# A hybrid attention encoder: tensor work of its projections moved from GpSimd to VectorE, buffers and one product order changed

## The chip, the cores and the metric

The kernel runs on one core of a Trainium2 chip. The metric is device time of one execution, in microseconds (us); the runs shown are whole executions, and one further execution was profiled. Engines are called PE (TensorE), DVE (VectorE), ACT (ScalarE), POOL (GpSimd) and SP (SyncE, which issues nearly all DMAs).

## The reference

One pre-norm layer with two parallel mixers, all in fp32. What the kernel's first stage has to produce is the projection of 2048 prompt rows and 128 sample rows (8 streams of 16):

```python
h = rms_norm(x, g_in)
proj = jnp.einsum('btd,de->bte', h, w_in)
qa, ka, va, z_a, qd, ckv_in, kpe_in, z_b, m_a, m_b = jnp.split(proj, SPLIT_POINTS, axis=-1)
qa = rope(qa.reshape(b, t, H_A, 2, DK_A), pos)
k_rows = rope(ka.reshape(b, t, H_A, 2, DK_A), pos).reshape(b, t, H_A, 2 * DK_A)
# y_a = W_oa(DiffAttn * silu(z_a)), y_b = W_ob(MLA * silu(z_b))
# x   = x + W_out(sigmoid(m_a) * y_a + sigmoid(m_b) * y_b)
```

Differential attention has 4 heads, latent attention (MLA) 4 heads; the sample streams attend to 2048 cached rows each.

## The kernel before, in words

Every fp32 operand of a matmul is split in two numbers of TensorE's faster fp32 format (`hi`, by an ACT cast, and `lo = x - hi`, by a subtraction, L113 to L115), and each product is three matmuls, hi by hi, hi by lo and lo by hi.

Five stages follow one another on PE: `_phase_a` (projections, 0 to 662 us), `_phase_a2` (latent and rope work with the gate products z, to about 950), `_phase_b` (prompt attention, to about 1850), `_sample` (the 8 sample streams, to about 2260) and `_phase_c` (output projections y and out, to the end).

Phase A treats the 2176 rows as three parts of 768, 768 and 640 columns of h transposed. For each part:
- `squares` and `factors`: six (five) loads of x rows (`xn`), ACT squares with sums, POOL turns the sums into `rs`, DVE makes diagonals `dg` (L187), and PE spreads them with a matrix of ones into bank `psr` (L188). ACT copies that to R. For parts 1 and 2 the squares are issued inside the first pairs of the part before, the factors after its pair number 7 (counted from 0).
- `load_part`: 16 tiles of xT are scaled by R (L202, DVE), cast (`xhi`, L204, ACT) and split (`xlo`, L205, POOL).
- `sums`: four differences of x blocks for the seven-product scheme (L215, DVE), each split into `S[0..3]` (L217 ACT, L218 DVE, for one of the four POOL).
- `v_block` (psv, 144 matmuls for 6 row tiles) and `kpe_block`.
- eleven pairs, in the order latent, then rope and gate four times, then two latents. A pair multiplies a 2 by 2 block of weights with a 2 by 2 block of h by seven products p1 to p7 of 12 matmuls each. `pair_weights` loads weights, makes four sums (L294, POOL, in part 0 only; they are stored to `wsum` in DRAM and loaded from there in parts 1 and 2) and splits the seven operands. `pair_products` adds the banks up on DVE (L325): v from p6, m1 from p2, u3 from p7, v and w from p5, v from p3, u3 from p4, in this order. A rope pair ends with four products by cosine and sine per half, two on POOL (L355, L357) and two on DVE (L356, L358).

Seven banks of PSUM rotate through these products, so a product may start when the adds on the bank seven allocations earlier are done. Temporaries come from one rotating pool `tmp` (12 buffers and some lent by another pool); the `dg` tiles are among them. The weight sums have one buffer (pool `a_q`). All engines run their instructions in the order in which a scheduler put them, from a cost model and priorities given by the order of the code; on each engine that order is fixed when the kernel is built.

In `_sample`, `diff_stream(b)` handles differential attention of stream b, `mla_streams(b)` latent attention of streams b and b+1; the last gate products z_13 to z_15 are placed between their matmuls. Names there: `ssd`, `atsd`, `posd`, `otsd` belong to a diff stream, `ktsm`, `ssm`, `posm`, `otsm` to MLA streams. Phase C starts with `y`, from `o` tiles that are loaded to `ox` and split.

Of the kernel before, what the change touches and what calls it, by code (L numbers as in the profile page):

```python
# [11 lines left out]
F32 = mybir.dt.float32  # L12
F32R = mybir.dt.float32r
BF16 = mybir.dt.bfloat16
AF = mybir.ActivationFunctionType
ALU = mybir.AluOpType
# [4 lines left out]
P = 128  # L21
D = 1024
SEQ = 2048
NB = 8
# [5 lines left out]
H = 4  # L30
# [6 lines left out]
NG = 384  # L37
GROUPS = [(t, min(NG, T - t)) for t in range(0, T, NG)]

PARTS = [(0, 384), (768, 384), (1536, 320)]  # L40
# [88 lines left out]
def _phase_a(c):  # L129

    nc, tc = c.nc, c.tc
    with (
        tc.tile_pool(name="a_h", bufs=1) as ph,
        tc.tile_pool(name="a_w", bufs=7) as pw,
        tc.tile_pool(name="a_s", bufs=2) as pst,
        tc.tile_pool(name="a_q", bufs=1) as pq,
        tc.tile_pool(name="a_t", bufs=12) as pt,
        tc.tile_pool(name="a_c", bufs=1) as pc,
        tc.tile_pool(name="a_p", bufs=7, space=PSUM) as pp,
# [13 lines left out]
        def tmp(n, name, m=P):  # L153
            return turn("t", 4, pt, c.zt).tile([P, NG], F32, tag="t", name=name)[:m, :n]
# [6 lines left out]
            [(c.zh if i == 0 else ph).tile([P, 4, 2 * NG], F32R, tag=f"{l}{i}", name=f"x{l}{i}") for l in ("hi", "lo")]  # L161
            for i in range(2)
        ]
        S = [[ph.tile([P, 4, NG], F32R, name=f"t{l}{i}") for l in ("h", "l")] for i in range(4)]

        R, ss = {}, {}

# [8 lines left out]
        def factors(p):  # L176
            t0, n = PARTS[p]
            nt = 2 * n // P
            R[p] = pc.tile([P, 2 * NG], F32, tag="R", name=f"R{p}", bufs=2)
            r = pc.tile([P, 8], F32, tag="rs", name=f"rs{p}", bufs=2)[:, :nt]  # L180
            _rsqrt(c, r, ss[p][:, :nt], 1.0 / D)
            for a in range(0, nt, 3):
                w = min(3, nt - a) * P
                ps = bank(f"psr{p}_{a}")
                for t in range(a, min(a + 3, nt)):
                    dg = tmp(P, f"dg{p}_{t}")
                    nc.vector.tensor_scalar(dg, c.ident, r[:, t : t + 1], None, op0=ALU.mult)  # L187
                    nc.tensor.matmul(ps[:, (t - a) * P : (t - a + 1) * P], c.ones, dg, start=True, stop=True)  # L188
                nc.scalar.copy(R[p][:, a * P : a * P + w], ps[:, :w])
            nc.sync.dma_start(c.Rh[:, t0 : t0 + 2 * n], R[p][:, : 2 * n])  # L190

        def load_part(p):
            t0, n = PARTS[p]
            raw = {}
            for j in range(4):
                for i in range(2):
                    kt = j + 4 * i
                    for half in range(2):
                        cut = slice(half * n, half * n + n)
                        x = tmp(n, f"x{p}_{kt}_{half}")  # L200
                        nc.sync.dma_start(x, c.i["xT"][:, kt, t0 + half * n : t0 + half * n + n])
                        nc.vector.scalar_tensor_tensor(x, x, c.g_in[:, kt : kt + 1], R[p][:, cut], op0=ALU.mult, op1=ALU.mult)  # L202
                        hi, lo = (z[:, j, cut] for z in X[i])
                        nc.scalar.copy(hi, x)  # L204
                        nc.gpsimd.tensor_tensor(lo, x, hi.bitcast(F32), op=ALU.subtract)  # L205
                        raw[j, i, half] = x
            return raw

        def sums(p, raw):
            n = PARTS[p][1]  # L210
            for j in range(4):
                b11, b12, b21, b22 = (raw[j, i, half] for i in range(2) for half in range(2))

                for i, out, x, y in ((0, b11, b12, b11), (2, b12, b22, b12), (1, b22, b22, b11), (3, b21, b21, b22)):
                    nc.vector.tensor_tensor(out, x, y, op=ALU.subtract)  # L215
                    hi, lo = (z[:, j, :n] for z in S[i])
                    nc.scalar.copy(hi, out)  # L217
                    (nc.gpsimd if i == 2 else nc.vector).tensor_tensor(lo, out, hi.bitcast(F32), op=ALU.subtract)  # L218

        def v_block(p):  # L220
            t0, n = PARTS[p]
# [43 lines left out]
        def kpe_block(p):  # L265

            t0, n = PARTS[p]
            st = stage([P, KT, 64], f"ws_kpe{p}")
            nc.sync.dma_start(st, c.i["wkpe"])
            w = operand([P, KT, P], f"w_kpe{p}")  # L270
            _split(nc, w[:, :, 0:64], w[:, :, 64:128], st)
            for half in range(2):
                ps = bank(f"ps_kpe_{p}_{half}")[:, :n]
                for kt in range(KT):
                    xh, xl = (z[:, kt % 4, half * n : half * n + n] for z in X[kt // 4])
                    nc.tensor.matmul(ps, w[:, kt, :], xh, start=(kt == 0), stop=False)
                    nc.tensor.matmul(ps, w[:, kt, :], xl, start=False, stop=(kt == KT - 1))
                t = tmp(n, f"kpe{p}_{half}")
                nc.scalar.copy(t, ps)
                nc.sync.dma_start(c.kpT[:, t0 + half * n : t0 + half * n + n], t)  # L280

        def pair_weights(p, u, nm):
            st = [stage([P, KT, P], f"ws_{nm}_{i}") for i in range(2)]
            nc.sync.dma_start(st[0], c.i["wu"][u])
            sums = pq.tile([P, 4, 4, P], F32, tag="s", name=f"s_{nm}")
            a11, a12 = (st[0][:, k : k + 4] for k in (0, 4))
            s1, s2, s3, s4 = (sums[:, i] for i in range(4))
            if p == 0:
                nc.sync.dma_start(st[1], c.i["wu"][u + 1])
                a21, a22 = (st[1][:, k : k + 4] for k in (0, 4))  # L290
                for out, x, y, op in (
                    (s1, a21, a22, ALU.add), (s2, s1, a11, ALU.subtract), (s4, a12, s2, ALU.subtract), (s3, a11, a21, ALU.subtract)
                ):
                    nc.gpsimd.tensor_tensor(out, x, y, op=op)  # L294
                nc.sync.dma_start(c.wsum[u // 2], sums)
            else:

                a22 = st[1][:, 4:8]
                nc.sync.dma_start(sums, c.wsum[u // 2])
                nc.sync.dma_start(a22, c.i["wu"][u + 1][:, 4:8])  # L300
            ops = []
            for i, x in enumerate((a11, a12, s4, s2, s3, s1, a22)):
                w = operand([P, KT, P], f"w{i}_{nm}")
                _split(nc, w[:, 0:4], w[:, 4:8], x)
                ops.append(w)
            return ops
# [10 lines left out]
        def pair_products(p, u, nm):  # L317

            n = PARTS[p][1]
            a11, a12, s4, s2, s3, s1, a22 = pair_weights(p, u, nm)  # L320
            one, two = slice(0, n), slice(n, 2 * n)
            m1, v, u3, w = (tmp(n, f"{x}{nm}") for x in ("m1", "v", "u3", "w"))

            def add(out, x, y):
                nc.vector.tensor_tensor(out, x, y, op=ALU.add)  # L325

            p1 = product(f"p1{nm}", a11, X[0], one)
            nc.scalar.copy(m1, p1)
            p2 = product(f"p2{nm}", a12, X[1], one)
            p3 = product(f"p3{nm}", s4, X[1], two)  # L330
            p6 = product(f"p6{nm}", s2, S[1], one)
            add(v, p6, m1)
            add(m1, p2, m1)
            p7 = product(f"p7{nm}", s3, S[2], one)
            add(u3, p7, v)
            p5 = product(f"p5{nm}", s1, S[0], one)
            add(v, p5, v)
            add(w, p5, u3)
            add(v, p3, v)
            p4 = product(f"p4{nm}", a22, S[3], one)  # L340
            add(u3, p4, u3)
            return (m1, v), (u3, w)

        def rope_pair(p, u, dst, pair, out, scale):
            t0, n = PARTS[p]
            res = pair_products(p, u, f"r{u}_{p}")
            for half in range(2):
# [4 lines left out]
                co, si = cs[:, 0], cs[:, 1]  # L352
                ta, tb = res[0][half], res[1][half]
                m1, m2, m3, m4 = (tmp(n, f"m{i}{nm}") for i in range(4))
                nc.gpsimd.tensor_tensor(m1, ta, co, op=ALU.mult)  # L355
                nc.vector.tensor_tensor(m2, tb, si, op=ALU.mult)  # L356
                nc.gpsimd.tensor_tensor(m3, tb, co, op=ALU.mult)  # L357
                nc.vector.tensor_tensor(m4, ta, si, op=ALU.mult)  # L358
                nc.vector.tensor_tensor(m1, m1, m2, op=ALU.subtract)
                nc.vector.tensor_tensor(m3, m3, m4, op=ALU.add)  # L360
# [37 lines left out]
        for p in range(len(PARTS)):  # L398
            raw = load_part(p)
            sums(p, raw)  # L400
            v_block(p)
            kpe_block(p)
            for i, f in enumerate(pairs(p)):
                f()
                if p + 1 < len(PARTS):
                    if i < 2 * PARTS[p + 1][1] // P:
                        squares(p + 1, i)
                    elif i == 7:
                        factors(p + 1)


# [329 lines left out]
def _sample(c, stack):  # L741
# [215 lines left out]

    for b in range(0, NB, 2):
        diff_stream(b)
        mla_streams(b)  # L960
        diff_stream(b + 1)


    ss, r = (p1.tile([P, H * SEQ // P], F32, name=f"rsub{i}") for i in range(2))
    flat = c.rsub.rearrange("h t -> (h t)").rearrange("(p r) -> p r", p=P)
    nc.sync.dma_start(ss, flat)
    for i in range(0, H * SEQ // P, 8):
        _rsqrt(c, r[:, i : i + 8], ss[:, i : i + 8], 1.0 / P)
    nc.sync.dma_start(flat, r)

    gz = big([P, 8, TS], "s_gz")
    nc.sync.dma_start(gz, c.gzT[:, :, new].rearrange("k p n -> p k n"))
# [478 lines left out]
```

## Time and profile before

| | us |
|---|---|
| three runs, lowest, median, highest | 2659.81, 2671.47, 2674.51 |
| profiled execution | 2666.7 |
| its span in the profile | 2664.9 |

| engine | PE | DVE | ACT | POOL |
|---|---|---|---|---|
| busy us | 2453.1 | 1629.3 | 1207.0 | 813.4 |
| share of the span | 92% | 61% | 45% | 31% |

The mean granted clock of PE is 0.968 of full speed (2.4 GHz); where the profile says 0.50, it is the lower level, 1.2 GHz. Shares are means over stages with different limits: DVE is busy for 80% of the first part of phase A. The idle time of PE is read stage by stage: what PE waited for, how often and how long.

### The profile page before, as it was taken

The page shows a single profiled execution, that of the slowest core. Times are in us where ns is not written, and L with a number is a line of the kernel's source. Part 1 is how long each engine was busy: PE and PEld are TensorE (multiplying, and loading weights), DVE is VectorE, ACT ScalarE, POOL GpSimd, SP SyncE. Part 2 cuts the span into 40 slices and gives each one's busy share as a digit, 9 for nine tenths or more (in the row PEclk, how much of TensorE's full clock was granted, in tenths as well). Part 3 has the DMA queues.
Part 4 walks back from the last instruction along what each step waited for, and adds up shares of the span by engine and source line. Part 5 has one row for each costly group of instructions (what it writes and reads, how often), then busy time and mean ns, then how long its engine had stood idle before and what let it go on. Part 6 is the DMA issues. An engine that isn't in the chain of part 4 may idle for free. (4 is left out here: it accounts for less than half of the span.)

```text
span 2664.9 us, 44262 instructions
## 1 busy us (share of the span) xinstructions
PE 2453.1 (92%) x15470; PEld 2166.9 (81%) x15470; DVE 1629.3 (61%) x3358; ACT 1207.0 (45%) x2996; POOL 813.4 (31%) x996
## 2 busy tenths in 40 slices
PE   6898898999788889999999999998999997999998
PEld 5798798898787879888998998786675774888887
DVE  7686777867665557887686677896333323433333
ACT  5443543444433356666575566775334333311111
POOL 6362411311533333344343334444101001122221
PEclk9999999999899899999999999999999998999999
DMA  5777577477767796576467657423887676534432
GB/s 196 238 271 242 182 245 243 155 233 240 233 204 254 241 285 213 186 238 198 145 186 219 215 176 226 141 76 122 344 329 294 256 303 212 173 130 130 127 112 93
DMA packets 303998, 553.29 MB, mean 208 GB/s; under 512 B 29184, under 2 KB 230176, under 8 KB 288544
## 3 DMA queue, kind: packets, MB, share of 16 engines
q1 hardware_dynamic: 303776, 550.46, 62.6%
q8 instruction: 123, 2.02, 0.3%
q14 instruction: 99, 0.81, 0.1%
HBM read 397.16 MB, written 153.19 MB: 207 GB/s over the span
## 5 line engine op out<-in xcount | busy, mean ns | idle before, releaser
L100 PE MATMUL z<-z_hi,zw 128*128 128x384 f32 (+1 forms) x768 | 264.9, 345 | 35.2 <-ACT zt L453 26.4
L102 PE MATMUL z<-z_hi,zw 128*128 128x384 f32 (+1 forms) x768 | 258.4, 336 | 3.1 <-DMA zw<-wz 2.9
L101 PE MATMUL z<-z_lo,zw 128*128 128x384 f32 (+1 forms) x768 | 258.9, 337 | 0.0
L1055 DVE TENSOR_REDUCE pmd<-sd 128x1 f32<-128x512 f32 (+3 forms) x320 | 189.7, 603 | 52.5 <-PE sd L1156 31.6
L1057 ACT ACTIVATE ed<-sd,pmd 128x512 f32<-128x512 f32 (+3 forms) x320 | 200.8, 631 | 43.7 <-DVE pmd L1055 29.4
L1096 POOL TENSOR_SCALAR ed<-ed,ad 128x512 f32<-128x512 f32 (+3 forms) x160 | 114.9, 733 | 293.8 <-DVE ad L1072 134.1
L1156 PE MATMUL sd<-k,q 128*128 128x512 f32 (+2 forms) x640 | 191.6, 386 | 3.2 <-ACT ed L1057 1.5
L100 PEld LDWEIGHTS z<-z_hi,zw 128*128 128x128 f32 x768 | 148.9, 194 | 54.4 <-ACT zt L453 32.8
L102 PEld LDWEIGHTS z<-z_hi,zw 128*128 128x128 f32 x768 | 148.5, 193 | 10.1 <-issue 4.6
L101 PEld LDWEIGHTS z<-z_lo,zw 128*128 128x128 f32 x768 | 148.9, 194 | 8.1 <-issue 6.3
L115 DVE TENSOR_TENSOR zw<-zs,zw 128x512 fp32r<-128x512 f32 x128 | 91.8, 746 | 95.2 <-ACT zw L114 91.3
L1096 POOL TENSOR_SCALAR em<-em,am 128x512 f32<-128x512 f32 (+3 forms) x160 | 104.4, 667 | 141.8 <-DVE am L1072 107.3
L100 PE MATMUL y<-o,wh_ab 128*128 128x384 f32 (+1 forms) x384 | 127.8, 333 | 9.1 <-DVE sm L1277 9.1
L1280 POOL TENSOR_TENSOR sm<-sm,sm 128x384 f32<-128x384 f32 (+1 forms) x48 | 48.1, 1003 | 267.4 <-DVE sm L1277 267.4
L102 PE MATMUL y<-o,wl_ab 128*128 128x384 f32 (+1 forms) x384 | 126.8, 331 | 0.3 <-DVE wl_ab L115 0.3
L101 PE MATMUL y<-o,wh_ab 128*128 128x384 f32 (+1 forms) x384 | 127.0, 331 | 0.0
L1057 ACT ACTIVATE em<-sm,pmm 128x512 f32<-128x512 f32 (+3 forms) x160 | 100.1, 628 | 58.7 <-DVE pmm L1055 46.3
L1114 DVE TENSOR_TENSOR ptld<-ptd,pthd 128x512 fp32r<-128x512 f32 (+3 forms) x160 | 96.2, 605 | 49.5 <-ACT pthd L1113 48.8
L1277 DVE SCALAR_TENSOR_TENSOR sm<-sm,y 128x384 f32<-128x384 f32 (+1 forms) x96 | 50.4, 530 | 117.1 <-PE y L102 117.0
L1055 DVE TENSOR_REDUCE pmm<-sm 128x1 f32<-128x512 f32 (+3 forms) x160 | 95.8, 604 | 34.3 <-PE sm L1199 21.0
L1282 ACT ACTIVATE m<-sm 128x384 fp32r<-128x384 f32 (+1 forms) x48 | 24.3, 506 | 202.6 <-POOL sm L1280 202.6
L1156 PEld LDWEIGHTS sd<-k,q 128*128 128x128 f32 x640 | 104.1, 191 | 13.2 <-ACT ed L1057 4.1
(510 smaller groups left out, 7845.9 us busy)
## 6 DMA issues: line engine op xcount, KB each, us to landing
zs<-in_wu_dram SPq DMA_DIRECT2D x64, 512.0 KB
zw<-wz SPq DMA_DIRECT2D x64, 512.0 KB
ksd<-in_ckT_dram SPq DMA_DIRECT2D x32, 1024.0 KB
vsd<-in_cv_dram SPq DMA_DIRECT2D x32, 1024.0 KB
q<-Qs SPq DMA_DIRECT2D x128, 128.0 KB
wz<-zw SPq DMA_DIRECT2D x32, 512.0 KB
ksm<-in_cc_dram SPq DMA_DIRECT2D x16, 1024.0 KB
smT<-zt SPq DMA_DIRECT2D x80, 192.0 KB
```

Source lines behind the costliest of these rows:

```text
L100: nc.tensor.matmul(out, ah, bh, start=(j == 0), stop=False)
L101: nc.tensor.matmul(out, ah, bl, start=False, stop=False)
L102: last = nc.tensor.matmul(out, al, bh, start=False, stop=(j == n - 1))
L115: nc.vector.tensor_tensor(lo, src, hi.bitcast(F32), op=ALU.subtract)
L1055: nc.vector.tensor_reduce(nm_, ps[:, :w], axis=AX.X, op=ALU.max, negate=True)
L1057: nc.scalar.activation(e[:, :w], ps[:, :w], AF.Exp, bias=nm_, accum_out=l[:, s, i : i + 1])
L1096: nc.gpsimd.tensor_scalar(p, p, a[:, 0, j : j + 1], 1.0, op0=ALU.mult, op1=ALU.mult)
L1114: nc.vector.tensor_tensor(ptl[ch][:, :n, i * P : (i + 1) * P], v, hi.bitcast(F32), op=ALU.subtract)
L1156: nc.tensor.matmul(ps[:, :n], qs[s][:, j, qc], ks[s].tiles[i][:, :n], start=(j == 0), stop=(j == 1 and not last))
L1277: nc.vector.scalar_tensor_tensor(s, s, 1.0, ps, op0=ALU.add, op1=ALU.mult)
L1280: nc.gpsimd.tensor_tensor(sm[0], sm[0], sm[1], op=ALU.add)
L1282: nc.scalar.mul(z[0], sm[0], 0.5)
```

## The change

- The POOL operations of phase A (`xlo` of L205, the one `tl` of L218, the weight sums of L294, two rope products of L355 and L357) are issued on DVE: 152 instructions.
- The pool of weight sums has two buffers.
- `dg` has three tiles of its own, and factors are issued after pair 6.
- The fourth sum of x blocks has no tiles of its own: after `kpe_block`, `last_sum` writes its split over the second half of X[0]; p4 reads it there. p4 stands behind p3, ahead of p6, p7 and p5; the halves of `kpe_block` are swapped.
- At the end of `_sample` the last `mla_streams` comes after the last `diff_stream`, and the block `rsub` after the first round of streams.

```diff
-        tc.tile_pool(name="a_q", bufs=1) as pq,
+        tc.tile_pool(name="a_q", bufs=2) as pq,
...
-        S = [[ph.tile([P, 4, NG], F32R, name=f"t{l}{i}") for l in ("h", "l")] for i in range(4)]
+        S = [[ph.tile([P, 4, NG], F32R, name=f"t{l}{i}") for l in ("h", "l")] for i in range(3)]
...
-                    dg = tmp(P, f"dg{p}_{t}")
+                    dg = pc.tile([P, P], F32, tag="dg", name=f"dg{p}_{t}", bufs=3)
...
-                        nc.gpsimd.tensor_tensor(lo, x, hi.bitcast(F32), op=ALU.subtract)
+                        nc.vector.tensor_tensor(lo, x, hi.bitcast(F32), op=ALU.subtract)
...
                     nc.vector.tensor_tensor(out, x, y, op=ALU.subtract)
-                    hi, lo = (z[:, j, :n] for z in S[i])
-                    nc.scalar.copy(hi, out)
-                    (nc.gpsimd if i == 2 else nc.vector).tensor_tensor(lo, out, hi.bitcast(F32), op=ALU.subtract)
+                    if i < 3:
+                        split(out, (z[:, j, :n] for z in S[i]))
+
+        def split(src, parts):
+            hi, lo = parts
+            nc.scalar.copy(hi, src)
+            nc.vector.tensor_tensor(lo, src, hi.bitcast(F32), op=ALU.subtract)
+
+        def last_sum(p, raw):
+            n = PARTS[p][1]
+            for j in range(4):
+                split(raw[j, 1, 0], (z[:, j, n : 2 * n] for z in X[0]))
...
-            for half in range(2):
+            for half in (1, 0):
...
-                    nc.gpsimd.tensor_tensor(out, x, y, op=op)
+                    nc.vector.tensor_tensor(out, x, y, op=op)
...
-            for i, x in enumerate((a11, a12, s4, s2, s3, s1, a22)):
+            for i, x in enumerate((a11, a12, s4, a22, s2, s3, s1)):
...
             p3 = product(f"p3{nm}", s4, X[1], two)
+            p4 = product(f"p4{nm}", a22, X[0], two)
...
-            p4 = product(f"p4{nm}", a22, S[3], one)
             add(u3, p4, u3)
...
-                nc.gpsimd.tensor_tensor(m1, ta, co, op=ALU.mult)
+                nc.vector.tensor_tensor(m1, ta, co, op=ALU.mult)
                 nc.vector.tensor_tensor(m2, tb, si, op=ALU.mult)
-                nc.gpsimd.tensor_tensor(m3, tb, co, op=ALU.mult)
+                nc.vector.tensor_tensor(m3, tb, co, op=ALU.mult)
...
             kpe_block(p)
+            last_sum(p, raw)
...
-                    elif i == 7:
+                    elif i == 6:
                         factors(p + 1)
...
         diff_stream(b)
-        mla_streams(b)
+        if b < NB - 2:
+            mla_streams(b)
         diff_stream(b + 1)
-
-
-    ss, r = (p1.tile([P, H * SEQ // P], F32, name=f"rsub{i}") for i in range(2))
...
+        if b == NB - 2:
+
+            mla_streams(b)
+        if b == 0:
+
+            ss, r = (p1.tile([P, H * SEQ // P], F32, name=f"rsub{i}") for i in range(2))
```

Three places in the order of instructions (the changed file's lines of phase A behind `sums` stand ten lower: L325 has become L335). The first is PE in part 0, around the fourth rope pair, where the factors of part 1 (`psr`, from `dg`) are spread. Before:

```order
L312 MATMUL p4r_0_1886<-th_146,w_r_0_1794 128x384
L313 MATMUL p4r_0_1886<-tl_147,w_r_0_1794 128x384
L314 MATMUL p4r_0_1886<-th_146,w_r_0_1794 128x384
L188 MATMUL psr_0_1948<-dg_0_1949,ones 128x128
L188 MATMUL psr_3_1959<-dg_3_1960,ones 128x128
L312 MATMUL p1g_0_2006<-xhi_136,w_g_0_1981 128x384
L313 MATMUL p1g_0_2006<-xlo_137,w_g_0_1981 128x384
```

Changed:

```order
L322 MATMUL p5g_0_1739<-th_140,w_g_0_1650 128x384
L323 MATMUL p5g_0_1739<-tl_141,w_g_0_1650 128x384
L324 MATMUL p5g_0_1739<-th_140,w_g_0_1650 128x384
L188 MATMUL psr_0_1768<-dg_0_1769,ones 128x128
L188 MATMUL psr_0_1768<-dg_1_1772,ones 128x128
L188 MATMUL psr_0_1768<-dg_2_1775,ones 128x128
L188 MATMUL psr_3_1779<-dg_3_1780,ones 128x128
L322 MATMUL p1r_0_1826<-xhi_136,w_r_0_1801 128x384
L323 MATMUL p1r_0_1826<-xlo_137,w_r_0_1801 128x384
```

The products of `psr` stood behind the fourth rope pair and now stand ahead of it; a pair ended with p4 and now ends with p5.

The second place is DVE in part 0, where the diagonals `dg` for part 1 stand (`m0r` to `m3r` are rope products, `w_l`, `w_r` weight splits, `csr` cosine and sine). Before, at the end of the fourth rope pair:

```order
L358 TENSOR_TENSOR m3r_0_1_1927<-vr_0_1798,csr_0_1_1922 128x384
L187 TENSOR_SCALAR dg_3_1960<-ident,rs_1945 128x128
L115 TENSOR_TENSOR w_l_0_2129<-s_l_0_2116,w_l_0_2129 128x512
L115 TENSOR_TENSOR w_l_0_2132<-s_l_0_2116,w_l_0_2132 128x512
L356 TENSOR_TENSOR m1r_0_0_1903<-u3r_0_1799,csr_0_0_1900 128x384
L356 TENSOR_TENSOR m1r_0_1_1925<-wr_0_1800,csr_0_1_1922 128x384
L187 TENSOR_SCALAR dg_0_1949<-ident,rs_1945 128x128
```

Changed, in the adds of the second rope pair (`s_g` is a weight sum):

```order
L335 TENSOR_TENSOR m1r_0_1150<-p2r_0_1168,m1r_0_1150 128x384
L115 TENSOR_TENSOR w_r_0_1454<-ws_r_0_0_1441,w_r_0_1454 128x512
L187 TENSOR_SCALAR dg_0_1769<-ident,rs_1765 128x128
L187 TENSOR_SCALAR dg_1_1772<-ident,rs_1765 128x128
L187 TENSOR_SCALAR dg_2_1775<-ident,rs_1765 128x128
L335 TENSOR_TENSOR u3r_0_1152<-p7r_0_1222,vr_0_1151 128x384
L115 TENSOR_TENSOR w_r_0_1460<-ws_r_0_1_1442,w_r_0_1460 128x512
L304 TENSOR_TENSOR s_g_0_1625<-ws_g_0_1_1623 128x512
L304 TENSOR_TENSOR s_g_0_1625<-ws_g_0_0_1622,ws_g_0_1_1623 128x512
```

The first three diagonals moved forward by two rope pairs, and weight sums stand among the adds.

The third place is PE at the end of the sample streams. Before, the gate product z_15 stands among MLA matmuls:

```order
L892 MATMUL ssm_1_24020<-kTsm_1_0_24021,sp 64x512
L100 MATMUL z_15_25658<-z_hi_25076,zw_4_15_25650 128x384
L101 MATMUL z_15_25658<-z_lo_25077,zw_4_15_25650 128x384
L102 MATMUL z_15_25658<-z_hi_25076,zw_4_15_25651 128x384
L100 MATMUL z_15_25658<-z_hi_25076,zw_4_15_25650 128x384
```

Changed, it ends ahead of them:

```order
L102 MATMUL z_15_25656<-z_hi_25074,zw_4_15_25649 128x384
L870 MATMUL otsd_24177<-ident,osd_24170 128x128
L891 MATMUL ktsm_0_0_0_24193<-ident,ksm_0_0_24190 128x128 x4
L891 MATMUL ktsm_0_0_1_24199<-ident,ksm_0_0_24190 128x128 x4
L891 MATMUL ktsm_0_1_0_24208<-ident,ksm_0_1_24205 128x128 x4
L891 MATMUL ktsm_0_1_1_24214<-ident,ksm_0_1_24205 128x128 x4
```

The last z went from the MLA streams to the last diff stream, and nothing of z is left beside the MLA matmuls.

## Rows read from the trace of the kernel before

**Rows 1.** Busy time by stretch: PE, PEld, DVE, ACT, POOL; then granted clock, DMA share, GB/s.

```profile
17.00:235.00 218.00, 184.96 (x945) 174.80 (x946) 174.01 (x255) 94.97 (x192) 121.73 (x83) 0.92 0.70 233
235.00:450.00 215.00, 192.38 (x1038) 185.33 (x1037) 157.08 (x262) 93.34 (x190) 55.65 (x38) 0.96 0.66 217
450.00:662.00 212.00, 196.66 (x1181) 189.32 (x1180) 157.19 (x275) 90.46 (x191) 40.02 (x36) 0.97 0.65 214
```

**Rows 2.** Waits of PE, 0 to 662 us: total us, times, longest.

```profile
PE psr L188 <- DVE dg L187: 39.0, 3, 17.7
PE psv L236 <- ACT xhi L204: 14.3, 4, 5.9
PE p2r L312 <- DVE vg L325: 11.2, 6, 3.3
PE p3r L312 <- ACT w_r L114: 9.1, 1, 9.1
PE p2r L312 <- DVE vl L325: 6.9, 1, 6.9
PE psv L238 <- POOL xlo L205: 3.1, 1, 3.1
```

**Rows 3.** Timeline of POOL: start, duration, [idle before, releaser].

```profile
93.08 1.26 POOL L294 TENSOR_TENSOR s_r<-ws_r 128x512 f32<-128x512 f32 x1 [24.43 <-DMA wsum<-s_l]
```

**Rows 4.** Timeline of DVE in the fourth rope pair.

```profile
224.99 0.29 DVE L187 TENSOR_SCALAR dg<-ident,rs 128x128 f32<-128x128 f32 x1 [1.44 <-DMA out_kT_dram<-m2r]
```

**Rows 5.** Stretches right behind PE's gaps, PE alone: busy, count, clock.

```profile
99.10:103.10 4.00, 3.95 (x11) 0.50 0.98 317
103.10:107.10 4.00, 4.00 (x24) 0.97 0.96 358
219.30:222.30 3.00, 2.95 (x11) 0.50 0.88 260
447.50:451.50 4.00, 3.94 (x14) 0.50 0.80 252
```

**Rows 6.** Groups of POOL's instructions, 0 to 662: busy, mean ns, idle before.

```profile
L205 POOL TENSOR_TENSOR xlo<-x,xhi 128x384 fp32r<-128x384 f32 (+1 forms) x48 | 59.1, 1255 | 96.9 <-ACT xhi L204 96.9
L355 POOL TENSOR_TENSOR m0r<-m1r,csr 128x384 f32<-128x384 f32 (+1 forms) x12 | 15.4, 1280 | 180.0 <-DVE m1r L325 180.0
L294 POOL TENSOR_TENSOR s_r<-ws_r,ws_r 128x512 f32<-128x512 f32 x4 | 6.2, 1557 | 0.0
```

**Rows 7.** Groups of DVE's instructions, 0 to 662 us.

```profile
L202 DVE SCALAR_TENSOR_TENSOR x<-x,vec,R 128x384 f32<-128x384 f32 (+1 forms) x48 | 47.0, 1013 | 3.8 <-DMA x<-in_xT_dram 3.8
L215 DVE TENSOR_TENSOR x<-x,x 128x384 f32<-128x384 f32 (+1 forms) x48 | 36.3, 770 | 0.0
L115 DVE TENSOR_TENSOR w_r<-s_r,w_r 128x512 fp32r<-128x512 f32 x48 | 36.0, 761 | 42.8 <-ACT w_r L114 42.8
L356 DVE TENSOR_TENSOR m1r<-u3r,csr 128x384 f32<-128x384 f32 (+1 forms) x12 | 15.9, 1321 | 0.0
```

**Rows 8.** Timeline of DVE, 188 to 192 us.

```profile
188.63 1.37 DVE L356 TENSOR_TENSOR m1r<-wr,csr 128x384 f32<-128x384 f32 x1
190.87 0.68 DVE L115 TENSOR_TENSOR w_r<-s_r,w_r 128x512 fp32r<-128x512 f32 x1
191.47 0.54 DVE L359 TENSOR_TENSOR m0r<-m0r,m1r 128x384 f32<-128x384 f32 x1
```

**Rows 9.** Timeline of POOL at the same time.

```profile
188.26 1.33 POOL L357 TENSOR_TENSOR m2r<-wr,csr 128x384 f32<-128x384 f32 x1
193.69 3.00 POOL L294 TENSOR_TENSOR s_g<-ws_g 128x512 f32<-128x512 f32 x1 [4.10 <-DVE w_r L115]
```

**Rows 10.** Timeline of ACT: the last square for part 1.

```profile
150.69 1.06 ACT L174 ACTIVATE xn<-xn 128x1024 f32<-128x1024 f32 x1 [6.52 <-DMA xn<-in_xn_dram]
```

**Rows 11.** Timeline of PE at the end of the sample streams.

```profile
2259.04 0.48 PE L859 MATMUL otsd<-ident,osd 128*128 128x128 f32 x1 [10.36 <-DVE osd L857]
```

**Rows 12.** Timeline of ACT ahead of that.

```profile
2256.82 0.51 ACT L114 CAST o<-ox 128x384 fp32r<-128x384 f32 x1 [1.48 <-POOL ox L1259]
2257.23 0.27 ACT L855 ACTIVATE osd<-posd 128x128 f32<-128x128 f32 x1
```

More of the change, by code (lines that the diff above doesn't have):

```diff
@@ L319, in pair_products @@
             n = PARTS[p][1]
-            a11, a12, s4, s2, s3, s1, a22 = pair_weights(p, u, nm)
+            a11, a12, s4, a22, s2, s3, s1 = pair_weights(p, u, nm)
             one, two = slice(0, n), slice(n, 2 * n)
@@ L959, in _sample @@
         diff_stream(b)
-        mla_streams(b)
+        if b < NB - 2:
+            mla_streams(b)
         diff_stream(b + 1)
-    ss, r = (p1.tile([P, H * SEQ // P], F32, name=f"rsub{i}") for i in range(2))
[L965 to L969, printed above, removed]
+        if b == NB - 2:
+            mla_streams(b)
+        if b == 0:
+            ss, r = (p1.tile([P, H * SEQ // P], F32, name=f"rsub{i}") for i in range(2))
+            flat = c.rsub.rearrange("h t -> (h t)").rearrange("(p r) -> p r", p=P)
+            nc.sync.dma_start(ss, flat)
+            for i in range(0, H * SEQ // P, 8):
+                _rsqrt(c, r[:, i : i + 8], ss[:, i : i + 8], 1.0 / P)
+            nc.sync.dma_start(flat, r)
     gz = big([P, 8, TS], "s_gz")
```

## The prediction

> **What bounds the kernel now.** I read the page first: PE is busy for 92% of the span, so the kernel is bound by PE, and all that an edit off PE can give back is PE's idle time and the slow clock behind it. I then read the stretches [rows 1], since the diff touches phase A and the last sample streams alone. The reader should see two things there. PE is idle for 645.0 - 574.0 = 71.0 us of the 645 us of phase A. And DVE is busy for 174.0, 157.1 and 157.2 us in the three parts, 488.3 in all, so 80% of part 0 and 73 to 74% of the others; POOL has 217.4, most of it in part 0. Third come PE's waits [rows 2], which say where these 71 us and the 17.7 before the first product lie: on `dg` three times (39.0 us, of which 17.7 is the start of the program, so 21.3 for the two later parts), on `xhi` at the start of psv (14.3), on adds of DVE ahead of p2 (11.2 and 6.9), once on a weight operand (9.1) and once on `xlo` (3.1). Last I followed two of them back. The operand of p3 came late because its weight sum started late: POOL waited 24.43 us for the store of the sum before, which had the only buffer [rows 3]. And diagonals came late because a `dg` stood on DVE waiting for a temporary that a store was still reading [rows 4].
>
> Behind each long gap PE runs at the lower of its two levels: clock 0.50 with 11 matmuls in 4.0 us, against 24 in the next 4.0 us [rows 5]. So a product of 12 matmuls takes 2.0 us at the upper level, and half of each slow stretch is lost.
>
> **The change part by part.**
>
> *Two buffers of sums.* The wait of 24.43 us has no cause any more, since the next sum has a buffer of its own. It gives back the 9.1 us and half of the slow stretch of about 4 us behind it: -11.1. What is late next is the sum itself, four additions on DVE among the adds, so the bounds are -11.1 and 0. I take -11.1, as these additions take a fraction of the 24.43 us.
>
> *Own tiles for dg, factors a pair earlier.* Two gaps, 21.3 us [rows 2], and half of the slow stretches of 3.0 and 4.0 us [rows 5], 3.5: -24.8. In the changed order the fourth `dg` needs the tile that the first `psr` product frees, a round trip that I put at 0.5 us a part, about the two short instructions of it: -23.8. The first three diagonals have moved forward by two rope pairs on DVE and wait there for `rs`, which hangs on the last square of an x tile. Today that square itself waits 6.52 us for its load [rows 10]. Behind the waiting `dg` stand the add of p7, weight splits and sums, and PE's next products wait for those. Bounds 0 and +6.5, I take +3.
>
> *POOL's tensor products on DVE.* POOL needs 1255, 1280 and 1557 ns for these [rows 6]. DVE needs 0.54 us for 384 columns and 0.68 for 512 where POOL is idle, as it is from 189.6 to 193.7 us [rows 8, 9]. The 152 are 48 xlo, 12 tl, 48 rope products and 44 sums: 108 x 0.54 + 44 x 0.68 = 88.2 us more for DVE. Against that, DVE's own instructions are slow beside POOL: the same kind of product took 1.37 us at 188.63 while POOL worked, and the means are 1013, 770 and 1321 ns [rows 7, 8, 9]. At 0.54 us each, 48 of L202 give back 22.7, 48 of L215 11.0, 24 of L356 (one group of 12 is shown, the other is like it) 18.7, and 251 weight and v splits at 0.08 us (761 - 680) 20.1: 72.5 us. The sum for DVE is 488.3 + 88.2 - 72.5 = 504 us, 83% of a phase A of some 610 us. It stays off the bound, just.
>
> The Trainium skill states this mechanism: GPSIMD Engine Reference, section 8 (Key points), says that GpSimd shares its SBUF interfaces with VectorE and that DVE instructions with two SBUF inputs are those that suffer. The trace agrees, with 1.37 beside POOL and 0.54 without. Section 4.1 (Engine selection) puts GpSimd at about half of VectorE's speed for two inputs; here it is 1255 to 540 ns. By that rule phase A has the 504 us of DVE above; without it the long means stay, which is the last rival below.
>
> For PE the move gives back the 3.1 us of xlo. At the start the six loads of x rows have six xT tiles among them (196 KB each, 1.18 MB), where two rope tables (0.79 MB) stood; 0.39 MB at the 317 GB/s of a busy stretch [rows 5] is 1.2 us later. So -1.9.
>
> The waits of p2 on adds, 18.1 us, have long DVE instructions in front of the add. Shorter ones remove some: bounds -18.1 and 0, I take half, -9.
>
> *p4 behind p3.* The products take as long as before, and the waits for the fourth sum (now made after `kpe_block`) are hidden by kpe's second half and p1 to p3, 3 products or 6 us ahead of the first p4. But the last product of a pair is now p5, with four adds behind it. Before, from the end of p5 to the next pair's p3, whose bank the add of p3 frees, there were p4, p1 and p2: 6 us. Now there are p1 and p2: 4 us. In that time DVE has to do the adds of p5 twice and of p3, 3 x 0.54, and what stands between them (a rope product, a sum, a split in the rope pairs): about 3.6 us. If DVE is late by more than 0.4 us there, PE waits. Nothing in the trace shows such a wait, so the nearest is that of p2: 11.2 us in 6 times, 1.9 each. Bounds 0 and 33 pairs x 1.9 = +63; I take a third of the 12 rope pairs, 4 x 1.9 = +7.5, nearer the lower end since the gate pairs, with no rope products, have room.
>
> *Last streams.* The last diff stream has been moved under z and the last MLA streams out of it. Today PE loses 10.36 us at `otsd` [rows 11], because the ACT instruction that frees it stands behind casts of `o` that wait for POOL [rows 12]; these casts stay ahead of the last streams' small steps, now those of MLA. That gap can go (-10.4), or come a second time (+10.4); I take 0, as the casts and their loads are the same. The block `rsub` stands at the same places of SP's order as before: 0.
>
> *Sum.* -11.1 - 23.8 + 3 - 1.9 - 9 + 7.5 = -35.3 us, so 2666.7 - 35.3 = 2631.4 for the profiled execution. That one lies 4.8 us below the median of the runs shown, 2671.5; against the median it is 2636.
>
> **Rivals.**
>
> *More comes back.* All 18.1 us of the p2 waits go, no p3 wait appears and `dg` waits for nothing: -11.1 - 24.8 - 1.9 - 18.1 = -56, and with the tail's gap gone -66: 2615 and 2605. For it: DVE's adds are the same 0.54 us work and only what stands before them shrinks. Against: in order engines with 83% load seldom lose no time.
>
> *Waits are replaced.* The first rope pairs of part 0 still wait for sums, now behind splits on DVE (0 for -11.1), the p2 waits stay (0), p3 and `dg` cost +7.5 and +6.5, and the tail costs its +10.4: -23.8 - 1.9 + 24.4 = -1, no change: 2670.
>
> *DVE misses the shorter deadline.* In each of the 33 pairs PE waits 1.9 us for the add of p3: +63 in place of +7.5, so -42.8 + 63 = +20: 2692, slower. It decides from 42.8 / 1.9 = 23 pairs on. For it: 11.2 and 6.9 us of waits on adds are there today with two more microseconds of room, and part 0 has 80% DVE load. Against: those waits are 7 in 33 pairs.
>
> *The long means are not POOL's doing.* Then DVE has 488.3 + 108 x 0.77 + 44 x 0.76 = 605 us, 94% of today's 645, and PE waits for it throughout: nothing gained, or slower by up to the 20 us above. Against it: rows at the same line with 1.37 and 0.54 us.
>
> **How the numbers follow.** The forecast has 0.55, more comes back 0.12, waits replaced 0.15, the deadline 0.12, long means 0.06. Under 0.5%, or 13 us, a measurement of this kernel can't tell a change from none. Faster by more than that: the first two and a little of the third (part of its terms not coming), 0.70. The same: most of the third and some of the last, 0.15. Slower: the deadline and the rest of the last, 0.15. The forecast's own range is 2620 to 2655. The range for all takes in the larger gain at the low end and at the high end the case of no change and a part of the slower ones: 2604 to 2678.
>
> **What would show it.** Right: no gap ahead of a `psr` after the start, none at the first p3r, POOL nearly idle up to 662 us; means near 0.54 us at L202 and at the rope products; DVE near 504 us in phase A, and the first y some 35 us earlier. Wrong: waits of p3 on DVE's v in many pairs, a DVE that stands for `rs` in the second rope pair, phase A as long as today, or a gap at the last MLA streams longer than the 10.4 us that went.

## The result and the profile after

The changed kernel takes 2603.45 us (median of 4 runs, 2598.38 to 2607.42) against 2667.98 for the kernel before in 4 runs: a ratio of 0.9759, 95% interval 0.9724 to 0.9793. It is 64 us faster, where 35 were forecast, and half a microsecond below the range.

The profiled execution shows where. Phase A runs up to the first z, which started at 692.2 us (30 us later than the 662 given above for the end of phase A) and now starts at 628.1, so phase A gave 64 us. Phase A2 gave 4 back, and the stretch from the last z to the first y gave 7; the other stages are within 2.5 us of before. Up to the first z PE is idle for 48.7 us instead of 95.5, and takes 579.4 instead of 596.7 for the work itself, as less of it falls on the slow clock. So 47 us are gaps and 17 us clock.

The stretches of phase A, with the columns of [rows 1]:

```profile
17.00:235.00 218.00, 205.35 (x1112) 196.29 (x1113) 188.31 (x363) 106.02 (x213) 2.63 (x3) 1.00 0.79 266
235.00:450.00 215.00, 205.51 (x1128) 198.27 (x1126) 163.71 (x317) 103.18 (x202) 1.41 (x2) 0.98 0.73 241
450.00:640.00 190.00, 176.47 (x1105) 170.47 (x1104) 146.11 (x304) 90.42 (x187) 10.10 (x9) 0.96 0.69 222
```

PE starts 1112 matmuls in the first of these instead of 945, at a granted clock of 1.00 instead of 0.92. The waits of PE up to 640 us, as in [rows 2] (those of z, in phase A2, left out):

```profile
PE psr L188 <- DVE dg L187: 21.0, 2, 18.5
PE psv L246 <- ACT xhi L204: 12.7, 4, 6.8
PE p3r L322 <- DVE m1g L335: 2.4, 2, 1.9
PE psv L246 <- ACT wv L114: 1.8, 1, 1.8
PE psv L247 <- DVE wv L115: 1.5, 1, 1.5
```

Of the 39.0 us for `dg` the start is left and 2.5 us; every wait of p2 on an add is gone, not half of them; so is that of p3 on its weight. The start of psv on `xhi` stays.

DVE's groups, which answer to [rows 7], and one that came from POOL:

```profile
L202 DVE SCALAR_TENSOR_TENSOR x<-x,vec,R 128x384 f32<-128x384 f32 (+1 forms) x48 | 26.3, 589 | 1.8 <-DMA x<-in_xT_dram 1.6 <-ACT R L189 0.2
L215 DVE TENSOR_TENSOR x<-x,x 128x384 f32<-128x384 f32 (+1 forms) x48 | 25.0, 528 | 0.0
L115 DVE TENSOR_TENSOR w_r<-s_r,w_r 128x512 fp32r<-128x512 f32 x48 | 32.8, 683 | 9.9 <-ACT w_r L114 9.9
L366 DVE TENSOR_TENSOR m1r<-u3r,csr 128x384 f32<-128x384 f32 (+1 forms) x12 | 6.3, 526 | 0.0
L205 DVE TENSOR_TENSOR xlo<-x,xhi 128x384 fp32r<-128x384 f32 (+1 forms) x48 | 23.8, 527 | 0.0
```

The mean of L202 fell from 1013 to 589 ns, of L215 from 770 to 528, of the rope product from 1321 to 526. The stretch up to the first z, in the kernel before and then in the changed one, with the columns of [rows 1]:

```profile
0.00:692.20 692.20, 596.70 (x3311) 571.88 (x3311) 506.20 (x824) 297.68 (x607) 229.17 (x178) 0.95 0.67 223
0.00:628.10 628.10, 579.37 (x3311) 557.61 (x3311) 493.36 (x977) 302.49 (x608) 14.16 (x26) 0.99 0.74 246
```

DVE is busy for 493.4 us in 977 instructions; it was 506.2 us in 824. The move cost DVE nothing.

### The profile page after: what moved, and what is told of

It is laid out like the page before. It is cut to its first block, busy times and chain, and to the rows that moved or that the text cites. A ratio compares the mean times of both kernels' runs of the same rounds, so it can differ in the third digit from the quotient of the medians.

```text
span 2596.6 us, 44017 instructions
## 1 busy us (share of the span) xinstructions
PE 2435.1 (94%) x15470; PEld 2153.6 (83%) x15470; DVE 1613.2 (62%) x3510; ACT 1212.1 (47%) x2996; POOL 599.5 (23%) x844
## 5 line engine op out<-in xcount | busy, mean ns | idle before, releaser
L443 POOL TENSOR_TENSOR z_lo<-zx,z_hi 128x384 fp32r<-128x384 f32 (+1 forms) x48 | 46.7, 1000 | 365.5 <-ACT z_hi L442 365.5
L1292 DVE SCALAR_TENSOR_TENSOR sm<-sm,y 128x384 f32<-128x384 f32 (+1 forms) x96 | 50.3, 529 | 116.6 <-PE y L102 116.6
L1128 ACT CAST pthd<-ptd 128x512 fp32r<-128x512 f32 (+3 forms) x160 | 82.6, 522 | 71.2 <-PE ptd L1125 70.0
```

The costliest lines, as they stand in the source:

```text
L1128: nc.scalar.copy(hi, v)
```

## The experiments

Times are ratios to the kernel before on the same chip, with their 95% interval; a microsecond figure is the ratio's difference times 2668. Theory A: DVE's instructions are slow because POOL works beside them, and PE waits for DVE. Theory B: the gain is in buffers and tiles that were waited for. Later expectations use letters anew and say themselves what each means. The changed kernel's own interval is 9 us to either side, so a difference of 10 us or less from it is not clear of noise.

**The engine move undone, and alone.** The changed kernel with `nc.gpsimd` in the 152 places:

```diff
-                        nc.vector.tensor_tensor(lo, x, hi.bitcast(F32), op=ALU.subtract)
+                        nc.gpsimd.tensor_tensor(lo, x, hi.bitcast(F32), op=ALU.subtract)
...
-                    nc.vector.tensor_tensor(out, x, y, op=op)
+                    nc.gpsimd.tensor_tensor(out, x, y, op=op)
...
-                nc.vector.tensor_tensor(m1, ta, co, op=ALU.mult)
+                nc.gpsimd.tensor_tensor(m1, ta, co, op=ALU.mult)
```

> The changed kernel with its 152 tensor products of phase A on POOL again (xlo, one tl, weight sums, two rope products); two buffers of sums, own dg tiles, p4 behind p3 and the order of the last streams stay. Theory A (the extra gain is DVE's own instructions, which are slow beside POOL): waits of PE on DVE's adds come back, 15 to 25 us in phase A, with slow clock behind them, and L202 and the rope products of DVE are near 1000 to 1300 ns again; 2630 to 2650 us. Theory B (the gain is in the buffers and the dg tiles, which take waits for slots away; the engine does not matter): within 8 us of the changed kernel's 2603, waits on adds under 5 us.

0.9945 (0.993 to 0.996), 2654 us: 50 us lost, a little more than theory A said; theory B falls. The means of L202 and of the rope product are 1057 and 1344 ns again, and the waits on adds are back:

```profile
PE p2r L322 <- DVE vg L335: 14.8, 2, 8.7
PE p2r L322 <- DVE vl L335: 6.1, 1, 6.1
```

And the kernel before with this move alone, the same lines in the other direction:

> The kernel before with the 152 tensor products of phase A on DVE and nothing else changed (one buffer of sums, dg among the temporaries, p4 last, old order of the last streams). Theory A (the faster DVE is most of the gain by itself, the rest comes from the buffers): 2667 less some 40, 2615 to 2640 us, POOL nearly idle, waits of p2 on adds under 5 us in all, DVE's busy time in phase A within 20 us of the 488 before. Theory E (the parts are worth something only together, since undoing each cost 9 to 51 us): 2645 us or more.

0.9796 (0.9772 to 0.982), 2615 us: 54 of the 64 us, by the move alone. PE's waits up to 640 us there:

```profile
PE psr L188 <- DVE dg L187: 31.0, 3, 16.8
PE psv L236 <- ACT xhi L204: 12.6, 3, 5.8
PE z L100 <- ACT zw L114: 8.4, 1, 8.4
PE p2l L312 <- DVE vg L325: 1.2, 1, 1.2
```

The p2 waits are gone but for 1.2 us, and of the 21.3 us ahead of `psr` 7.1 went without a tile of its own for `dg`. The 9.1 us of p3 went too, with one buffer of sums still. SP's timeline tells why, in the kernel before and then in this one:

```profile
87.83 0.40 SPq L295 DMA_DIRECT2D wsum<-s_l  x1
```

```profile
50.43 0.38 SPq L295 DMA_DIRECT2D wsum<-s_l  x1
```

The store that freed the buffer stood behind all 36 stores of v of part 0; here it stands behind three of them. So waits that the prediction gave to three edits went, in whole or in part, with one. Theory E falls.

**POOL's work without the work.** The changed kernel, in which DVE keeps all it has, with additions on POOL that nobody needs:

```diff
+            scr = pc.tile([P, 4, P], F32, tag="scr", name=f"scr_{nm}")
+            for _ in range(6):
+                nc.gpsimd.tensor_tensor(scr, s1, s2, op=ALU.add)
             return ops
```

> The changed kernel with six more additions on POOL in each of the 33 pairs, which read two of the pair's weight sums and write a scratch tile that nobody reads. DVE has the same instructions as in the changed kernel. Theory A (DVE is slowed by POOL's work itself): DVE's mean for 128x512 splits rises from about 685 ns to 800 or more, DVE's busy time in phase A by 60 to 120 us, and PE waits on adds: 2615 to 2650 us. Theory B (only dependences count): DVE's means stay, 2600 to 2610 us.

1.0064 (1.0042 to 1.0087), 2684 us: 81 us slower than the changed kernel, more than theory A said, and slower than the kernel before. Up to the first z, which is at 713.3 us here, DVE is busy for 625.4 us in the same 977 instructions, 132 us more:

```profile
0.00:713.30 713.30, 606.02 (x3311) 578.58 (x3311) 625.41 (x977) 300.49 (x608) 327.98 (x224) 0.94 0.65 216
```

Groups of DVE up to 640 us:

```profile
L115 DVE TENSOR_TENSOR w_r<-s_r,w_r 128x512 fp32r<-128x512 f32 x47 | 44.9, 955 | 6.1 <-ACT w_r L114 6.1
L202 DVE SCALAR_TENSOR_TENSOR x<-x,vec,R 128x384 f32<-128x384 f32 (+1 forms) x48 | 26.3, 588 | 3.3 <-DMA x<-in_xT_dram 3.0 <-ACT R L189 0.2
L369 DVE TENSOR_TENSOR m1r<-u3r,csr 128x384 f32<-128x384 f32 (+1 forms) x11 | 16.8, 1526 | 0.0
L338 DVE TENSOR_TENSOR vg<-p6g,m1g 128x384 f32<-128x384 f32 (+1 forms) x10 | 5.3, 530 | 0.0
```

L202 runs where POOL has nothing to do and keeps its 588 ns; splits and rope products run in the pairs, beside POOL, and take 955 and 1526. The adds of a PSUM bank run in the pairs too and keep their 530 ns: what comes late is the instruction in front of an add, not the add. And the waits on adds are back:

```profile
PE psr L188 <- DVE dg L187: 34.6, 3, 17.9
PE p2r L325 <- DVE vg L338: 27.6, 6, 9.5
```

The extra additions also read the sums and so hold their buffers longer. But no wait of PE in the pairs is on a cast of a weight operand, and a held buffer would not lengthen DVE's instructions.

**The move in parts.** Of the lines of the first experiment, the rope products, the sums, and the splits of x alone:

> The changed kernel with the 48 rope products (two of four in each half) on POOL again. Theory A: POOL works beside the two rope products of DVE, which come back to 1200 to 1300 ns, right where DVE has the adds of the next pair behind them; a third of the 51 us or more: 2618 to 2635 us, waits on adds in rope and gate pairs. Theory F (the weight sums are what costs, as they stretch over whole pairs): 2603 to 2612 us.

> The changed kernel with the 44 weight sums of part 0 on POOL again (two buffers). Only part 0 can be touched. Theory A: about 70 us of POOL beside the weight splits and adds of part 0, 2615 to 2630 us, all of it in part 0. Theory F (the sums are what costs): 2630 us or more. If POOL's long instructions do nothing to DVE: 2600 to 2608 us.

> The changed kernel with xlo (48) and the split of one x sum (12) on POOL again. Undoing the rope products cost 6 us, the sums 14, all 152 together 51. If the parts add up (theory A as a plain sum): 2603 + 31 = 2634 us, lost at the three starts of the parts, psv in part 0 some 10 us longer. Theory G (POOL's work hurts more than in proportion, as its queue is in order and its pieces wait for each other): 2608 to 2622 us, and the rest of the 51 comes only when all three are there.

Ratios 0.9785 (0.9762 to 0.9808), 0.9814 (0.9792 to 0.9836) and 0.9825 (0.9808 to 0.9843): 7, 15 and 18 us above the changed kernel's ratio, 39 together, against 50 for all. The rope products land in theory F's range, the sums in theory A's, the splits at the upper edge of theory G's: no group carries it alone. Whether the parts add up is open: by these ratios they make 39 of 50 us, by the start of the first z in the profiles (638.3, 645.5 and 657.2 us, and 676.4 with all) 57 of 48. With the splits back, the last psv of part 0 starts 10 us later, with a wait of 8.1 us in the block, and waits on adds appear in pairs:

```profile
PE psv L247 <- DVE wv L115: 8.1, 1, 8.1
PE p2r L322 <- DVE vl L335: 5.9, 1, 5.9
PE p2g L322 <- DVE vr L335: 4.5, 1, 4.5
```

**One buffer of sums.** `bufs=1` for `a_q`:

> The changed kernel with one buffer of weight sums. Theory A (the second buffer is worth what the prediction gave it, the one wait of 9.1 us and its slow clock): 2603 + 11 = 2614 us, with one long gap of PE in part 0. Theory C (with the sums on DVE a sum that waits for the store of the sum before stops DVE's whole queue, adds included): several gaps of PE in part 0, together 25 to 80 us, 2630 to 2690.

0.9792 (0.9777 to 0.9806), 2612 us: 9 us, the size of theory A though not clear of noise, and not by its wait. No wait of PE on a weight above 0.4 us came back. Up to the first z the profile has 7.7 us more of idle time, 4.6 of them ahead of `psr`, and 6.5 us more of work on the slow clock. What theory C feared is there once: DVE stood for the store, but PE had products left.

```profile
86.61 0.69 DVE L304 TENSOR_TENSOR s_r<-ws_r 128x512 f32<-128x512 f32 x1 [11.77 <-DMA wsum<-s_l]
```

By its size theory C falls.

**The diagonals.** In the changed kernel `dg = tmp(P, ...)` and `i == 7` again; and the kernel before with own tiles and `i == 6` alone:

> The changed kernel with dg in the rotating temporaries and factors after pair 7 again. Theory A (the two gaps of 10.5 and 10.8 us come from the place and the slots of dg): both gaps come back with 3.5 us of slow clock, +22 to +27, 2625 to 2630 us. Theory D (they came from temporaries held long by slow rope products beside POOL, so the faster rope alone removed them): gaps ahead of psr under 5 us each, within 8 us of 2603.

> The kernel before with own tiles for dg and factors after pair 6, nothing else. The prediction's term alone: two gaps of 21.3 us and slow clock, -23.8, 2643 us. Rival (undoing it in the changed kernel cost 12 us, the rest being given back in a later wait or coming from slow rope products): -12 or less, 2655 us or more.

0.9797 (0.9779 to 0.9815) and 0.992 (0.9907 to 0.9934). In the changed kernel the edit is worth 10 us, between theories A and D, since the engine move had already taken a part; in the kernel before 21 us, near the 23.8 of the sum. The waits ahead of `psr` in the first run, then in the second:

```profile
PE psr L188 <- DVE dg L187: 30.8, 3, 17.0
```

```profile
PE psr L188 <- DVE dg L187: 30.9, 3, 18.2
PE psv L237 <- DVE wv L115: 8.1, 1, 8.1
```

Behind the start that is 13.8 and 12.7 us, where the kernel before had 21.3, the kernel with the move alone 14.2 and the changed one 2.5. So the engine move alone and this edit alone each leave more than half of these gaps, and only both together remove nearly all. The 21 us of the second run are then not the term's waits alone: 8.6 us of those went, and with them the 9.1 us of p3, since the store of `s_l` is issued at 67.59 us there, ahead of the stores of v; 8.1 us in psv of part 0 came anew.

**p4 last again.** Product, operand and add behind p5, operand in X[0]:

```diff
-            p4 = product(f"p4{nm}", a22, X[0], two)
...
             add(v, p3, v)
+            p4 = product(f"p4{nm}", a22, X[0], two)
             add(u3, p4, u3)
```

> The changed kernel with p4 again behind p5, its operand split last and its add last; the fourth sum still in the second half of X[0]. The prediction's term (with p4 behind p3 the next pair's p3 has 4 us instead of 6 for the adds of the pair before): waits of p3 on adds, 2.4 us in the changed kernel, go, and nothing else changes: 2600 to 2606 us. Rival (p4 last keeps its bank and its add late, so p4 waits take the place): waits on adds of 5 to 20 us, 2608 to 2625.

0.9758 (0.9729 to 0.9787), 2602 us: no difference within the noise. p4's place is worth nothing that these runs can tell, and of the 2.4 us of p3 waits 0.2 are left.

**The last streams.** The old order of the last lines in `_sample`:

> The changed kernel with the old order of the last streams. The prediction had 0 for it; the trace has 7 to 8 us less between the end of the last z and the first y. If the order does that: 2608 to 2612 us with a gap of some 10 us at the last otsd. If it is chance of what loads at that time: 2600 to 2606 us.

0.9769 (0.9754 to 0.9785), 2607 us, between the two expectations; the interval overlaps the changed kernel's. The profiles tell more: from the last z to the first y it is 56.2 us, against 49.8. In the old order, then in the changed kernel:

```profile
2198.23 0.48 PE L870 MATMUL otsd<-ident,osd 128*128 128x128 f32 x1 [10.68 <-DVE osd L868]
```

```profile
2172.41 2.82 PE L946 MATMUL atsm<-ident,esm 128*128 128x128 f32 x12 [4.04 <-POOL esm L935]
2193.01 1.22 PE L994 MATMUL ov<-s_olT,s_wv 128*128 128x128 f32 x4 [3.13 <-DVE s_gz L997]
```

The gap of 10.4 us of [rows 11] went with the order, and two of 4.0 and 3.1 took its place. The other profiles bear out the 6 us of that stretch: it is 55.6 to 56.8 us in all four with the old order, and 49.8 to 50.3 in all ten with the new one.

**A version that keeps the old start.** Own tiles of `dg` changed what the scheduler put first. With `dg` of part 0 among the temporaries, and own tiles for parts 1 and 2:

```diff
-                    dg = pc.tile([P, P], F32, tag="dg", name=f"dg{p}_{t}", bufs=3)
+                    dg = tmp(P, f"dg{p}_{t}") if p == 0 else pc.tile([P, P], F32, tag="dg", name=f"dg{p}_{t}", bufs=3)
```

> The changed kernel with dg of part 0 alone among the rotating temporaries, own tiles for parts 1 and 2. On SP the weights of v are then loaded ahead of the xT tiles, as before, with no xT tile among the x rows. With all dg among the temporaries psv of part 0 ended at 58.3 us, in the changed kernel at 63.4. If that comes from the order of these loads: 4 to 6 us faster than the changed kernel, 2597 to 2600. If not: 2601 to 2606 us.

0.9736 (0.9722 to 0.975), 2599 us, the fastest here; its interval overlaps that of the changed kernel. SP's timeline in the changed kernel, then in this one:

```profile
6.63 1.59 SPq L201 DMA_DIRECT2D x<-in_xT_dram  x2
9.20 0.33 SPq L173 DMA_DIRECT2D xn<-in_xn_dram  x1
16.77 0.85 SPq L237 DMA_DIRECT2D wsv<-in_wv_dram  x2
```

```profile
6.42 1.61 SPq L173 DMA_DIRECT2D xn<-in_xn_dram  x2
8.97 6.10 SPq L237 DMA_DIRECT2D wsv<-in_wv_dram  x4
```

With the weights of v loaded from 9.0 us instead of 16.8, the first `psr` comes 1.5 us earlier and the last psv of part 0 starts at 56.8 us instead of 63.4. The time goes the way of the expectation, but the overlap leaves open how much of this the program keeps.

## Why the prediction was wrong

The way was right and the main mechanism too: the contention of DVE and POOL was named, with the means that DVE's instructions would fall to. DVE's load came near the forecast 504 us (188.3 + 163.7 + 146.1 = 498 from 17 to 640 us), in part by luck: the sum let it rise by 16 us, and over the same work, from 17 us to the first z, it fell from 505.2 to 493.2. The size of the gain was off by a factor of nearly two. The step that failed is "The waits of p2 on adds, 18.1 us, have long DVE instructions in front of the add. Shorter ones remove some: bounds -18.1 and 0, I take half, -9", and with it the whole term of the engine move, -1.9 - 9 = -10.9 us; measured alone it is -54. The profile of the move alone shows what the term lacked: up to its first z, at 638.0 us, PE is idle for 54.6 us instead of 95.5, and its work takes 583.4 instead of 596.7. So 41 us are gaps (some 21 on DVE's adds, 9 on the weight of p3, 8 ahead of `psr`, 3 on xlo) and 13 us slow clock; the term had 9 and 3.1 of gaps, no clock, and 1.2 for the start against them. How much comes from shorter instructions and how much from the new order that the scheduler gave them is not separated. Step by step:

- *Sums, -11.1.* The second buffer is worth 9 in the changed kernel, not clear of noise, and the wait of 9.1 us that the term was made from goes with the engine move alone, and with the `dg` edit alone, by an earlier store.
- *dg, -23.8 and +3.* Alone 21, but that the size agrees is luck: 8.6 of the 21.3 us went and other waits made up the rest. The +3 did not come: the square ran at 126.3 us, and the early diagonals waited for nothing:

```profile
129.46 0.67 DVE L187 TENSOR_SCALAR dg<-ident,rs 128x128 f32<-128x128 f32 x3
```

- *Engine move, -10.9.* All 18.1 us went, not half. With them went slow clock: the sum had 2 + 3.5 us of clock for three gaps and none for the others; measured for the whole change are 17.
- *p4, +7.5.* 2.4 us of p3 waits came, and no time that the runs can tell. The sum took the waits of p2 as price, but these went with the engine move of the same change.
- *Last streams, 0.* Some 6 us by the profiles.
- *Start, -1.9.* The first `psr` came 0.8 us later, where 1.2 were worked out for the loads. The sum left out the later weights of v, with which psv of part 0 ends 6.6 us later than in the version that keeps the old start; 4 us of time lie between the two medians, not clear of noise.

The rival "more comes back" had 2605 to 2615 and 0.12, and its mechanism is what happened: the p2 waits went, the gaps ahead of `psr` went but for 2.5 us, and only 2.4 us of p3 waits came. That its 2605 lies so near 2603 is luck in part, since it has no slow clock for the p2 waits, 10.4 us for the tail that gave 7, and nothing for the 4 us that phase A2 gave back. The Trainium skill's rule (GPSIMD Engine Reference, section 8, Key points), that VectorE's instructions with two SBUF inputs are among those that contend with GpSimd, agrees with the groups above: 955 and 1526 ns beside POOL against 683 and 526, and 530 for adds with an input in PSUM.

## What to carry to other kernels

When work leaves an engine that slows another one, price the other engine's instructions by their mean where the first is idle, and set the moved work against what they get back; here DVE's busy time even fell by 13 us. Every wait that hangs on the freed engine then belongs to that one term, together with the slow clock behind it. And before an edit is given a wait of its own, ask whether another edit of the same change already removes it, or whether both are needed, as with the gaps ahead of `psr`.

## What the runs showed of the hardware

In the run with POOL's extra additions, an instruction of DVE can be sorted by whether it overlaps one of POOL (by more than 0.05 us). Of the 128x512 splits before the first z, 134 do not and take 680 ns on average; 126 do and take 1268. Of the 128x384 adds with an input in PSUM, 55 do not and take 543 ns; 99 do and take 547. So only the first kind, with both inputs in SBUF, is slowed.

Up to the first z POOL has 328.0 - 14.2 = 314 us more there than in the changed kernel, DVE 625.4 - 493.4 = 132 us more for unchanged work, 0.42 us for each of POOL's, and the time grew by 81 us, 0.26 for each. The kernel before had 229.2 - 14.2 = 215 us of POOL more than the changed one; at that rate, as an estimate, this is 55 us of time, near the 54 that the move gave.
